# RMSNorm with SiLU on one core: loads and stores trade their issuing engines, and each is issued at another moment

## The chip, the cores and the metric

The kernel runs on one core of a Trainium2 chip, and the program uses no other. The metric is the time of one execution on the device, in microseconds (us). Times are medians over several executions; a profile belongs to one execution, and its "span" (first to last instruction) is some 2 us shorter than the time. All profiled executions used here are fast, with a granted clock of 1.0.

## The reference

```python
x: (8, 1024, 2048) float32, gamma: (2048,), eps = 1e-5
rms = sqrt(mean(x ** 2, axis=-1, keepdims=True) + eps)
out = gamma * x / rms
result = out * (1 / (1 + exp(-out)))          # SiLU, float32
```

The input is 67.1 MB, and so is the output.

## The kernel before

The 8192 rows are cut into 16 blocks of 512 rows. A block is one tile of 128 partitions by 4 rows of 2048 numbers (4.194 MB), loaded by one transfer, worked on in place, and stored by one transfer. Six such tiles exist. VectorE takes the sums of squares of two rows of a block and does all scaling; ScalarE takes the other two sums, the square root and the SiLU. The parts that the change touches:

```python
J = 4
BUFS, LEAD = 6, 6
...
pool = ctx.enter_context(tc.tile_pool(name="pool", bufs=BUFS))
...
def load(b):
    xt = pool.tile([P, J * d], f32, name="xt")
    nc.sync.dma_start(out=xt, in_=xb[b])            # SyncE issues loads
    blocks[b] = xt

def sums(b, after_first=()):
    # ... VectorE: two tensor_tensor_reduce (cut)
    for j in range(na):
        nc.scalar.activation(out=junk_a, in_=row(b, j), func=ACT.Square,
                             accum_out=ss[:, j:j + 1])
        if j == 0:
            for s in after_first:
                store(s)                            # behind the first Square of block b
    # ... ScalarE: Sqrt (cut)

def finish(b, halves=False):
    for j in range(J):
        # VectorE: row * rstd * gamma (cut); after each second row:
        #   ScalarE: Silu over two rows; if halves: store those two rows
        ...

def store(b):
    nc.scalar.dma_start(out=ob[b], in_=blocks[b])   # ScalarE issues stores
    if b + LEAD < nblk:
        load(b + LEAD)                              # waits on SyncE for that store's landing

# gamma: 8 KB into a borrowed tile of the pool, spread to all partitions by TensorE (cut)
for b in range(1, last - 1):
    sums(b + 1, after_first=[b - 1])
    finish(b)
    invert(b + 1)
store(last - 2)
finish(last - 1)
store(last - 1)
sums(last)
invert(last)
finish(last, halves=True)
```

Waits aren't written by hand: an instruction that touches a tile waits for the instruction or transfer that has to be done with it. The wait stands on the engine that issues: in the kernel before, SyncE waits for stores to land in ten of its loads, 222.1 us in all.

## Time and profile before

| | before |
|---|---|
| time, median (lowest to highest), 3 runs | 317.37 us (317.27 to 317.58) |
| span of the profiled execution | 316.3 us (its time: 318.03 us) |
| VectorE, ScalarE busy | 223.5 us, 223.8 us (71% each) |
| two DMA queues, share of 16 engines' span | 49.7% and 49.2% |
| load, issue to landing (median) | 42.0 us |
| store, issue to landing (median) | 35.2 us |

Two habits help in reading it. First, the view puts a packet's whole time and all its bytes down to the stretch in which it starts, so that a short stretch can exceed 1.00. The DMA share tells whether packets were in flight, and only the rate in GB/s tells whether bytes flow as fast as they can. Second, "issue to landing" is mostly time in a queue: a block needs 4.194 MB / 433 GB/s = 9.7 us of the DMA engines, not 42.

### The profile page before, as it was taken

What the parts mean: (1) busy time and instruction counts of PE and PEld (TensorE: products, weight loads), DVE (VectorE), ACT (ScalarE), POOL (GpSimd) and SP (SyncE); (2) the same over time, 40 slices, a digit from 0 to 9 for tenths busy, and PEclk for the clock granted to TensorE, in tenths of its full rate; (3) what the DMA queues carried; (4) which work ended last, traced back from release to release, by engine and by line L of the source; (5) the groups of instructions that cost most, each with busy time, mean ns of one, the idle gap of its engine ahead of it and who ended that gap; (6) DMA issues with size and microseconds to landing.
All of it is one profiled execution on the core that took longest, in us unless ns stands there. A gap on an engine that the chain in (4) does not pass through costs nothing.

```text
span 316.3 us, 444 instructions
## 1 busy us (share of the span) xinstructions
PE 2.1 (1%) x8; PEld 0.5 (0%) x8; DVE 223.5 (71%) x147; ACT 223.8 (71%) x144; POOL 0.2 (0%) x4
## 2 busy tenths in 40 slices
PE   0200000000000000000000000000000000000000
PEld 0000000000000000000000000000000000000000
DVE  0679499999493983939849397593966939993900
ACT  1357958999967777678676687676786776879540
POOL 0000000000000000000000000000000000000000
DMA  8999999999999999999999999999999999999996
GB/s 328 402 464 410 452 390 410 452 419 443 439 424 452 411 452 410 452 414 456 406 456 414 448 414 448 439 423 452 414 452 410 452 414 456 406 456 410 452 407 269
DMA packets 4763, 134.25 MB, mean 425 GB/s; under 512 B 532, under 2 KB 532, under 8 KB 536
## 3 DMA queue, kind: packets, MB, share of 16 engines
q1 hardware_dynamic: 2304, 67.11, 49.7%
q10 hardware_dynamic: 2456, 67.12, 49.2%
q14 instruction: 3, 0.02, 0.0%
HBM read 67.12 MB, written 67.11 MB: 424 GB/s over the span
## 4 chain that ended last, share of the span: by engine, by line
DMA 74%; DVE 14%; ACT 5%; issue 2%; DVEq 1%; ACTq 0%; SPq 0%
DMA xt<-in_x_dram 44%; DMA out_dram<-xt 30%; DVE xt L84 11%; ACT xt L88 3%; DVE junk_v L64 3%; ACT junk_a L68 1%; DVEq L164 1%; ACT L74 0%; ACT rms L74 0%; DVE rstd L79 0%; ACTq L93 0%; DVE ss L64 0%; SPq L52 0%; DVEq L64 0%; ACTq L74 0%
## 5 line engine op out<-in xcount | busy, mean ns | idle before, releaser
L84 DVE SCALAR_TENSOR_TENSOR xt<-xt,rstd,g 128x2048 f32<-128x2048 f32 x64 | 146.2, 2347 | 0.1
L88 ACT ACTIVATE xt<-xt 128x4096 f32<-128x4096 f32 x32 | 115.4, 3615 | 36.8 <-DVE xt L84 36.7
L64 DVE CUSTOM_DVE_ANT_0 junk_v<-xt 128x2048 f32<-128x2048 f32 x32 | 73.5, 2298 | 56.1 <-DMA xt<-in_x_dram 55.5
L68 ACT ACTIVATE junk_a<-xt 128x2048 f32<-128x2048 f32 x32 | 60.1, 1879 | 29.2 <-DMA xt<-in_x_dram 28.3
L74 ACT ACT_TABLE_LOAD x15 | 19.2, 1283 | 9.9 <-DVE ss L64 9.9
L88 ACT ACT_TABLE_LOAD x15 | 19.2, 1283 | 3.1 <-DVE xt L84 2.9
L79 DVE RECIPROCAL rstd<-rms 128x4 f32<-128x4 f32 x16 | 2.8, 172 | 11.3 <-ACT rms L74 11.3
L114 DVE COPY g<-junk_v 128x2048 f32<-128x2048 f32 x1 | 2.3, 2292 | 9.2 <-PE junk_v L112 9.2
L68 ACT ACTIVATION_READ_ACCUMULATOR junk_a<-xt 128x1 f32 x32 | 6.0, 186 | 0.0
L74 ACT ACTIVATE rms<-ss,eps_t 128x4 f32<-128x4 f32 x16 | 4.8, 297 | 1.2 <-DVE ss L64 1.1
L64 DVE DVE_READ_ACCUMULATOR2_ANT ss<- 128x1 f32 x32 | 4.5, 141 | 0.0
L112 PE MATMUL junk_v<-xt,ones 1*128 1x512 f32 x8 | 2.1, 1133 | 8.1 <-DMA xt<-in_gamma_dram 8.1
L107 ACT ACT_TABLE_LOAD x1 | 1.3, 1283 | 0.7 <-PEq L150 0.7
L105 DVE MEMSET ones<- 128x128 f32 x1 | 0.2, 165 | 0.8 <-PEq L150 0.8
L112 PEld LDWEIGHTS junk_v<-xt,ones 1*128 1x128 f32 x8 | 0.5, 306 | 8.1 <-issue 8.1
L107 ACT ACTIVATE junk_a<-ones 128x1 f32<-128x1 f32 x1 | 0.2, 174 | 0.0
L150 POOL MEMSET const-uint8-127<- 128x1 uint8 x1 | 0.1, 102 | 0.0
L150 POOL MEMSET const-bfloat16-1.0<- 128x1 bf16 x1 | 0.1, 101 | 0.0
L150 POOL MEMSET const-float32-0.0<- 128x1 f32 x1 | 0.1, 98 | 0.2 <-issue 0.2
L150 POOL MEMSET const-float32-1.0<- 128x1 f32 x1 | 0.1, 98 | 0.0
L106 DVE MEMSET eps_t<- 128x1 f32 x1 | 0.1, 59 | 0.0
## 6 DMA issues: line engine op xcount, KB each, us to landing
xt<-in_x_dram SPq DMA_DIRECT2D x16, 4096.0 KB, 42.0
out_dram<-xt ACTq DMA_DIRECT2D x15, 4096.0 KB, 35.2
out_dram<-xt ACTq DMA_DIRECT2D x2, 2048.0 KB, 10.4
xt<-in_gamma_dram ACTq DMA_DIRECT2D x1, 8.0 KB
```

What stands on the lines that cost most here:

```text
L64: nc.vector.tensor_tensor_reduce(out=junk_v, in0=row(b, j), in1=row(b, j), scale=1.0, scalar=0.0, op0=ALU.mult, op1=ALU.add, accum_out=ss[ ...
L68: nc.scalar.activation(out=junk_a, in_=row(b, j), func=ACT.Square, accum_out=ss[:, j:j + 1])
L74: nc.scalar.activation(out=rms, in_=ss, func=ACT.Sqrt, scale=1.0 / d, bias=eps_t)
L79: nc.vector.reciprocal(out=rstd, in_=rmss.pop(b))
L84: nc.vector.scalar_tensor_tensor(out=row(b, j), in0=row(b, j), scalar=rstds[b][:, j:j + 1], in1=g, op0=ALU.mult, op1=ALU.mult)
L88: nc.scalar.activation(out=blocks[b][:, cols], in_=blocks[b][:, cols], func=ACT.Silu)
L105: nc.vector.memset(ones, 1.0)
L107: nc.scalar.activation(out=junk_a[:, 0:1], in_=ones[:, 0:1], func=ACT.Square)
L112: nc.tensor.matmul(junk_v[:, c * w:(c + 1) * w], ones[k:k + 1, :], grow[k:k + 1, 0:w], start=True, stop=True)
L114: nc.vector.tensor_copy(out=g, in_=junk_v)
L150: nc = _bacc.Bacc("TRN2", target_bir_lowering=False, num_devices=1)
L164: with _tile.TileContext(nc) as tc:
```

## The change

The intent: the engine that waits for a store's landing shall be ScalarE, which issues the next load where it is needed, and a store shall go out as soon as its SiLU is done, from SyncE, which has nothing else to do. Loads are tied to landings: load b+3 stands behind the first Square of block b+1, "the block two in front of it".

```diff
-    BUFS, LEAD = 6, 6
+    BUFS = 6
...
+    Q = 4
+    w = d // Q
+    grow = singles.tile([P, w], f32)
...
     def load(b):
         xt = pool.tile([P, J * d], f32, name="xt")
-        nc.sync.dma_start(out=xt, in_=xb[b])
+        nc.scalar.dma_start(out=xt, in_=xb[b])
...
                 for s in after_first:
-                    store(s)
+                    load(s)
...
     def store(b):
-        nc.scalar.dma_start(out=ob[b], in_=blocks[b])
-        if b + LEAD < nblk:
-            load(b + LEAD)
+        nc.sync.dma_start(out=ob[b], in_=blocks[b])
...
-        for b in range(BUFS - 1):
+        for b in range(BUFS):
             load(b)
...
-        nc.scalar.dma_start(out=grow[0:P:P // Q, 0:w], ...)
+        nc.sync.dma_start(out=grow[0:P:P // Q, :], ...)
...
-        load(BUFS - 1)
...
         finish(0)
+        store(0)
...
         for b in range(1, last - 1):
-            sums(b + 1, after_first=[b - 1])
+            sums(b + 1, after_first=[b + 3] if BUFS <= b + 3 < nblk else [])
             finish(b)
+            store(b)
             invert(b + 1)
-        store(last - 2)
```

(The two half stores of the last block move from ScalarE to SyncE too.)

More of the change, by code (lines that the diff above doesn't have):

```diff
@@ L89, in finish @@
                 if halves:
-                    nc.scalar.dma_start(out=ob[b][:, cols], in_=blocks[b][:, cols])
+                    nc.sync.dma_start(out=ob[b][:, cols], in_=blocks[b][:, cols])
     def store(b):
-        nc.scalar.dma_start(out=ob[b], in_=blocks[b])
-        if b + LEAD < nblk:
-            load(b + LEAD)
+        nc.sync.dma_start(out=ob[b], in_=blocks[b])
     with tc.manual_schedule():
-        Q = 4
-        w = d // Q
-        grow = pool.tile([P, J * d], f32, name="xt")
-        for b in range(BUFS - 1):
+        for b in range(BUFS):
             load(b)
@@ L107 @@
         nc.scalar.activation(out=junk_a[:, 0:1], in_=ones[:, 0:1], func=ACT.Square)
-        nc.scalar.dma_start(out=grow[0:P:P // Q, 0:w],
-                            in_=bass.AP(tensor=gamma.tensor, offset=gamma.offset, ap=[[w, Q], [1, w]]))
+        nc.sync.dma_start(out=grow[0:P:P // Q, :],
+                          in_=bass.AP(tensor=gamma.tensor, offset=gamma.offset, ap=[[w, Q], [1, w]]))
         for c in range(Q):
             k = c * (P // Q)
-            nc.tensor.matmul(junk_v[:, c * w:(c + 1) * w], ones[k:k + 1, :], grow[k:k + 1, 0:w],
+            nc.tensor.matmul(junk_v[:, c * w:(c + 1) * w], ones[k:k + 1, :], grow[k:k + 1, :],
                              start=True, stop=True)
         nc.vector.tensor_copy(out=g, in_=junk_v)
-        load(BUFS - 1)
         last = nblk - 1
```

## The prediction

> **What bounds the kernel now.** I read the page first, for which engine is full. Its third part lists the DMA queues: packets, megabytes, and the time of their packets as a share of the span of 16 DMA engines.
>
> ```profile
> DMA  8999999999999999999999999999999999999996
> GB/s 328 402 464 410 452 390 410 452 419 443 439 424 452 411 452 410 452 414 456 406 456 414 448 414 448 439 423 452 414 452 410 452 414 456 406 456 410 452 407 269
> ...
> q1 hardware_dynamic: 2304, 67.11, 49.7%
> q10 hardware_dynamic: 2456, 67.12, 49.2%
> ```
>
> Two queues carry 67.1 MB each (the input once, the output once) and together fill 49.7 + 49.2 = 98.9% of the DMA engines' time; VectorE and ScalarE are each busy for only 71% (223.5 and 223.8 us). Every slice but the first and the last is at 90% or more. So the question is not who issues, but whether the DMA engines ever run dry, and at what rate they work. For that I asked for the rate in stretches of my choice: start, loads alone, first store, steady state, stores alone, end. The last two columns are the DMA share and GB/s.
>
> ```profile
> 0.00:12.00 12.00, 2.09 (x8) 0.55 (x8) 1.94 (x3) 1.46 (x2) 0.20 (x4) 1.00 0.87 350
> 12.00:36.00 24.00, 0.00 (x0) 0.00 (x0) 19.19 (x14) 17.37 (x12) 0.00 (x0) 1.00 1.01 437
> 36.00:44.00 8.00, 0.00 (x0) 0.00 (x0) 5.70 (x6) 6.85 (x10) 0.00 (x0) 1.00 1.00 385
> ...
> 142.00:219.50 77.50, 0.00 (x0) 0.00 (x0) 55.20 (x36) 56.41 (x36) 0.00 (x0) 1.00 1.00 433
> ...
> 278.20:300.00 21.80, 0.00 (x0) 0.00 (x0) 16.65 (x11) 16.81 (x10) 0.00 (x0) 1.00 1.00 433
> 300.00:308.00 8.00, 0.00 (x0) 0.00 (x0) 1.09 (x1) 3.83 (x2) 0.00 (x0) 1.00 0.95 409
> 308.00:313.00 5.00, 0.00 (x0) 0.00 (x0) 0.00 (x0) 0.00 (x0) 0.00 (x0) 1.00 0.99 426
> 313.00:316.30 3.30, 0.00 (x0) 0.00 (x0) 0.00 (x0) 0.00 (x0) 0.00 (x0) 1.00 0.08 35
> ```
>
> Loads alone run at 437 GB/s, loads and stores mixed at 433, stores alone at 433. The total is therefore about the same whatever the mix, and only stretches below some 432 GB/s can be won back. Each loses its length times (1 - rate/432): the start 12 x (1 - 350/432) = 2.3 us, the stretch in which the first store begins 8 x (1 - 385/432) = 0.9 us, 300 to 308 us 0.4 us, the end 0.1 + 3.3 x (1 - 35/432) = 3.1 us. That is 6.7 us in the whole span of 316.3 us, and 5.4 us of it are the start of the first transfer and the landing of the last.
>
> Last, the timeline in the steady state, which shows who waits for whom within a block (start, us, engine, what; in brackets the idle time before it and what ended it).
>
> ```profile
> 195.35 3.62 ACT L88 ACTIVATE xt<-xt 128x4096 f32<-128x4096 f32 x1 [0.91 <-DVE xt L84]
> ...
> 200.81 1.88 ACT L68 ACTIVATE junk_a<-xt 128x2048 f32<-128x2048 f32 x1 [1.85 <-DMA xt<-in_x_dram]
> 200.87 0.34 ACTq L93 DMA_DIRECT2D out_dram<-xt  x1
> ```
>
> The Square of the next block starts when its load lands; such Squares stand at 181.46, 200.81 and 220.16 us, so a block takes 19.35 us, which is 2 x 4.194 MB / 19.35 us = 433.5 GB/s: the DMA's own pace. The last Silu of a block ends at 195.35 + 3.62 = 198.97 us, 17.5 us after the landing at 181.46, and ScalarE then idles 1.85 us for the next landing. Its store is issued only at 200.87, behind that landing.
>
> **What the Trainium skill says.** The page "DMA: Bandwidth & Descriptors" bears on this in three places. Its section "Issuing engines are not separate DMA queues" says that DMAs begun by different engines run on the same 16 DMA engines and interleave; trading queues then gives no bandwidth. The trace agrees so far: two queues at 49.7% and 49.2% add to one full set. "Where 436 GB/s comes from" puts the ceiling of the ports at 435 GB/s; the 433 measured in the steady state is within 0.5% of it (the same section's limit of about 358 for HBM isn't what this trace shows with one core at work). "Queues, rings and completion order" says that each DMA engine takes turns between the queue rows with work, packet by packet. In the trace a block of loads takes about 9.7 us alone (4.194 MB at 433 GB/s) and 19.35 us beside stores, which fits equal turns. The same page, under "Anatomy of one DMA — SWDGE (gpsimd) path", says that waits on semaphores happen on the issuing sequencer before dispatch. No view of before tests this for a load on ScalarE, but it is the danger of the change: there, a load that waits for a buffer's old store holds up ScalarE's arithmetic too.
>
> **The change part by part.**
> (1) Stores move to SyncE, right behind the last Silu. In the steady state each goes 200.87 - 198.97 = 1.9 us earlier, store 0 about 4 us earlier (its Silu ends at 32.70 us, it was issued at 36.67). The DMA engines are full at both moments, so this reorders bytes and adds no room: 0 us.
> (2) Loads move to ScalarE. Ten of them stand in the loop behind a Square, where 13 of the 17 stores stood. An issue costs the sequencer about 0.33 us in either place (0.34 for a store in the timeline, 328 ns median for a load), and ScalarE issues 16 loads in place of 17 stores and gamma. ScalarE has 1.85 us idle per block. 0 us.
> (3) A load is now tied to a landing as well as to a free buffer. Do the queues run dry? Load b+3 is issued just behind the landing of block b+1, when block b+2 is still to come: one whole block, 19.35 us of work beside stores or 9.7 us alone. ScalarE would have to be that late before the load queue emptied. In the start-up it is late by the most: block 4's Square comes after block 2's Silu, at some 67 us, and load 6 with it (before: 61.4 us). By my count from the rates block 5 then still has about 0.8 of a block to load, so nothing empties.
> (4) Does load b+3 wait for store b-3? A buffer's round takes 6 x 19.35 = 116.1 us. Before: store 35.2 (median to landing) + load 42.0 + from landing to store issue 220.22 - 181.46 = 38.8, sum 116.0: closed, no slack, SyncE simply waits for the store. After: load 2 x 19.35 = 38.7, holding 19.35 + 17.6 = 36.9, which leaves 116.1 - 75.6 = 40.5 us for the store. With two stores in the queue it takes 35.2 us, at worst 2 x 19.35 = 38.7. So 2 to 5 us to spare: the wait should be over when ScalarE comes to it.
> (5) Gamma gets a tile of its own and goes out on SyncE at once. Before, VectorE's copy of gamma ended at 12.5 us, ahead of the first block at 13.1 us; loads precede it in a different queue in both kernels. Load 5 no longer waits for it, but four loads were queued in front anyway. 0 us.
> (6) The start of the stores. Store 0 now lands near 55 us, and store 1 can't be issued before its Silu ends at about 56 us; so the store queue starts up twice, where before it started once. If each start loses up to the 0.9 us seen at 36 to 44 us, this adds 0 to 0.9 us, and I take 0.2.
> (7) The end hangs on the landing of block 14 (258.88 us) and the compute behind it: last half store issued 304.77 - 258.88 = 45.9 us later, which no part changes. 0 us.
> Sum: 317.4 + 0.2 = 317.6 us.
>
> **The rivals.**
> A. The wait moves onto ScalarE and stops the arithmetic. For it: the spare time in (4) is only a few us. Against it: while ScalarE is stopped, stores b-3 to b-1 and load b+2 are queued, so the DMA engines work on; the loss comes only at the end, if the last stores are issued late. I put this at 1 to 3 us, 318.5 to 320.5.
> B. Earlier stores fill bubbles and the kernel gets faster. For it: up to 1.3 us of the 6.7 us (the stretches at 36 and 300 us) aren't start or end latency. Against it: the steady state is at 433 GB/s with none to fill. At best 316.
> C. The store queue, now shallower, runs empty in every block, and starting it again costs rate each time. For it: the dip at the first store. Against it: by (4) the store queue should stay close to two deep. If it cost 0.3 us on each of 12 blocks, 321.
>
> **Range and chances.** The centre is 317.6. B bounds it below at about 316, A above at about 319 to 320; executions agree within 0.1% (317.27 to 317.58). I give 316.0 to 319.4. Faster by 2% would be 311.0, that is 6.3 of the 6.7 us that are not at full rate, most of them fixed latency: 0.01. Slower by 2% is 323.7 and needs C at twice the size, or a stall that I don't see: 0.03. Within 2%: 0.96.
>
> **What would show it.** Right: the two queues still fill some 99% of the DMA engines, mixed stretches at 432 to 434 GB/s, Squares 19.35 us apart, and ScalarE idle for about 1.9 us per block until a load lands. Store issue to landing stays near 35 us, and load issue to landing falls from 42 to near 38.7 us. For (4): no wait on ScalarE's queue for a store's landing in the loop. Rival A shows as such waits and a last half store issued later than 305 us; B as a rate above 420 GB/s at 36 to 44 us; C as a store landing time near 20 us and a steady rate clearly below 433 GB/s. The prediction is wrong if the mixed rate itself depends on which queue holds the deeper backlog, for which before has no contrast.

## The result, and the profile after

The changed kernel takes 317.23 us (317.16 to 317.56, 6 runs), the kernel before on the same chip 317.48 us (317.27 to 317.81, 6 runs). The ratio is 0.9993, with a 95% interval of 0.998 to 1.0006: the same. A ratio here is always the mean time of one kernel's fast runs over the mean of the other's fast runs of the same rounds, so not quite the ratio of the medians quoted.

The page of the changed kernel: busy tenths and rate of the DMA engines in 40 slices, and the two queues.

```profile
DMA  8999999999999999999999999999999999999997
GB/s 334 408 458 408 391 458 408 458 408 458 408 459 408 459 408 453 412 458 412 453 412 453 420 445 424 445 420 445 428 437 428 441 433 433 441 424 441 424 418 314
...
q10 hardware_dynamic: 2304, 67.11, 49.8%
q1 hardware_dynamic: 2456, 67.12, 49.4%
```

The queues have traded names (q10, with 2304 packets, now carries the loads), and that is all: 49.8 + 49.4 = 99.2%, against 98.9%. The rate over the same stretches as before (the last two columns are DMA share and GB/s):

```profile
0.00:12.00 12.00, 2.09 (x8) 0.55 (x8) 1.89 (x3) 1.46 (x2) 0.20 (x4) 1.00 0.87 350
12.00:36.00 24.00, 0.00 (x0) 0.00 (x0) 19.24 (x14) 17.41 (x12) 0.00 (x0) 1.00 1.04 437
36.00:44.00 8.00, 0.00 (x0) 0.00 (x0) 5.74 (x6) 6.85 (x10) 0.00 (x0) 1.00 0.91 393
44.00:64.00 20.00, 0.00 (x0) 0.00 (x0) 19.97 (x13) 16.19 (x11) 0.00 (x0) 1.00 1.01 437
...
142.00:219.50 77.50, 0.00 (x0) 0.00 (x0) 55.20 (x36) 56.41 (x36) 0.00 (x0) 1.00 1.00 433
...
300.00:308.00 8.00, 0.00 (x0) 0.00 (x0) 1.24 (x1) 3.98 (x2) 0.00 (x0) 1.00 0.95 410
```

They are the same stretches with the same rates: 350, 437, 433, 410. Only the stretch of the first store moved, from 385 to 393 GB/s, and that is no reading: the same view gives this kernel 459 GB/s when the edges are moved by 1 us, to 37 and 45 us. Over 12 to 64 us the two kernels have 429 and 430 GB/s. The profiled span is 1.2 us shorter than before (315.1 against 316.3), but that execution of before took 318.03 us, some 0.6 us above the median of its kind, so no gain of 1.2 us is to be read from it.

In the steady state of the changed kernel, the timeline shows the same block as before:

```profile
195.99 3.62 ACT L91 ACTIVATE xt<-xt 128x4096 f32<-128x4096 f32 x1 [0.91 <-DVE xt L87]
...
201.46 1.88 ACT L71 ACTIVATE junk_a<-xt 128x2048 f32<-128x2048 f32 x1 [1.85 <-DMA xt<-in_x_dram]
201.47 0.33 ACTq L55 DMA_DIRECT2D xt<-in_x_dram  x1
```

ScalarE again ends its SiLU (195.99 + 3.62 = 199.61 us), idles 1.85 us, and starts the next Square when the load lands. The only difference is what follows the landing: a load on its queue where a store stood. The list of who waited for whom, in which the total, the number of times and the longest are given, confirms that ScalarE didn't pay for its new duty:

```profile
ACT xt L91 <- DVE xt L87: 39.2, 28, 3.6
ACT junk_a L71 <- DMA xt<-in_x_dram: 26.2, 11, 7.9
```

In the whole list no instruction of ScalarE waits for a store's landing, and the last half store is issued at 304.91 us (before: 304.77), not later than 305 us as rival A would have it.

### The profile page after: what moved, and what is told of

It reads as the page before. It is cut to its first block, busy times and chain, and to the rows that moved or that the text cites. A ratio compares the mean times of both kernels' runs of the same rounds, so it can differ in the third digit from the quotient of the medians.

```text
span 315.1 us, 438 instructions
## 1 busy us (share of the span) xinstructions
PE 2.1 (1%) x8; PEld 0.5 (0%) x8; DVE 223.6 (71%) x147; ACT 223.7 (71%) x144; POOL 0.2 (0%) x4
## 3 DMA queue, kind: packets, MB, share of 16 engines
q10 hardware_dynamic: 2304, 67.11, 49.8%
q1 hardware_dynamic: 2456, 67.12, 49.4%
## 4 chain that ended last, share of the span: by engine, by line
DMA 65%; DVE 18%; ACT 10%; issue 2%; DVEq 1%; ACTq 0%
DMA xt<-in_x_dram 65%; DVE xt L87 13%; ACT xt L91 6%; DVE junk_v L67 4%; ACT junk_a L71 2%; ACT L77 2%; DVEq L161 1%; ACT L91 0%; ACT rms L77 0%; DVE rstd L82 0%; DVE ss L67 0%; DVEq L67 0%; ACTq L77 0%
## 5 line engine op out<-in xcount | busy, mean ns | idle before, releaser
L91 ACT ACTIVATE xt<-xt 128x4096 f32<-128x4096 f32 x32 | 115.5, 3616 | 39.2 <-DVE xt L87 39.2
L67 DVE CUSTOM_DVE_ANT_0 junk_v<-xt 128x2048 f32<-128x2048 f32 x32 | 73.6, 2299 | 56.6 <-DMA xt<-in_x_dram 55.9
L71 ACT ACTIVATE junk_a<-xt 128x2048 f32<-128x2048 f32 x32 | 60.1, 1879 | 26.7 <-DMA xt<-in_x_dram 26.2
L109 PE MATMUL junk_v<-grow,ones 1*128 1x512 f32 x8 | 2.1, 1132 | 8.1 <-DMA grow<-in_gamma_dram 8.1
## 6 DMA issues: line engine op xcount, KB each, us to landing
xt<-in_x_dram ACTq DMA_DIRECT2D x16, 4096.0 KB, 38.7
out_dram<-xt SPq DMA_DIRECT2D x15, 4096.0 KB, 34.6
```

The lines of the kernel that those rows point to most:

```text
L67: nc.vector.tensor_tensor_reduce(out=junk_v, in0=row(b, j), in1=row(b, j), scale=1.0, scalar=0.0, op0=ALU.mult, op1=ALU.add, accum_out=ss[ ...
L91: nc.scalar.activation(out=blocks[b][:, cols], in_=blocks[b][:, cols], func=ACT.Silu)
L109: nc.tensor.matmul(junk_v[:, c * w:(c + 1) * w], ones[k:k + 1, :], grow[k:k + 1, :], start=True, stop=True)
```

## The experiments

My theory: the DMA engines' rate is the whole time. As long as each DMA engine has bytes queued, neither the issuing engine nor the moment of issue nor a wait on an engine with slack matters. The rivals are those of the prediction: the wait hurts on ScalarE (A), earlier stores win something that something else loses (B), starting a queue anew costs rate (C). Twelve kernels ran, in three batches of four; each was timed in 3 rounds against the kernel before on the same chip. The medians of before in the batches were 317.46, 317.62 and 317.53 us.

| kernel | median, us | ratio to before (95%) |
|---|---|---|
| no arithmetic, old issue | 317.53 | 0.9995 (0.9978 to 1.0011) |
| no arithmetic, new issue | 317.10 | 0.9987 (0.9972 to 1.0002) |
| before, stores early | 317.38 | 0.9993 (0.9978 to 1.0008) |
| changed, stores late | 317.61 | 1.0029 (0.9983 to 1.0074) |
| changed, 5 buffers | 317.60 | 1.0002 (0.9987 to 1.0017) |
| before, 5 buffers | 317.84 | 1.0003 (0.9984 to 1.0021) |
| changed, load one landing later | 329.16 | 1.0371 (1.0337 to 1.0404) |
| changed, store queue started anew | 331.33 | 1.0437 (1.0406 to 1.0469) |
| before, 4 buffers | 328.53 | 1.0343 (1.0320 to 1.0366) |
| changed, 4 buffers | 335.01 | 1.0524 (1.0450 to 1.0597) |
| changed, one queue, gamma behind the loads | 365.73 | 1.1507 (1.1486 to 1.1528) |
| changed, one queue, gamma apart | 320.52 | 1.0091 (1.0074 to 1.0107) |

### Is there anything beside the transfers? The arithmetic taken out

```diff
-        sums(0) ... finish(last, halves=True)
+        for b in range(nblk):
+            store(b)                       # old: loads on SyncE, stores on ScalarE
+        # new: store(b) on SyncE, then load(b + 3) on ScalarE
```

The output is x itself and wrong.

> All arithmetic between load and store is taken out (the output is wrong on purpose: it is x itself); loads on SyncE and stores on ScalarE as before. Theory (the DMA engines' rate is the whole time, everything else hides beside it): 134.2 MB at 433 GB/s plus some 3.5 us of start and landing, a span of 313 to 316 us, that is 0.988 to 1.0 of before. Rival (waits between arithmetic and transfers cost a few per cent that some order of issue could win back): clearly below, 305 us or less.

> The same without arithmetic, with loads on ScalarE and stores on SyncE (output wrong on purpose). Theory: as the other copy within 0.3%, since both queues feed the same DMA engines. Rival (the queue that carries the loads matters): they differ by over 0.5%.

Measured: 317.53 and 317.10 us. The span of the first is 315.9 us, above the 313 or so of my lowest expectation but inside the range. The page of the copy with the old issue:

```profile
DMA  8999999999999999999999999999999999999996
...
q1 hardware_dynamic: 2304, 67.11, 49.7%
q10 hardware_dynamic: 2312, 67.12, 49.2%
...
HBM read 67.12 MB, written 67.11 MB: 425 GB/s over the span
```

A kernel that computes nothing takes as long as either kernel. So all 224 us of work on VectorE and on ScalarE, and every wait between them, are hidden in both, and no other order of the arithmetic around these transfers can win more than noise. (Orders of the transfers themselves were tried only in these two forms, and smaller first or last transfers, which might shorten the start and the end, not at all.) The copies differ from each other by less than their intervals, though their transfers queue very differently (store issue to landing 42.7 us in one, 28.8 us in the other). This is the strongest single result: rival B is out for this change. Neither kernel has anything left above its own transfers.

### One part alone: the early stores

```diff
 # in the kernel before: store(b) no longer behind the Square of block b+2, but
             finish(b)
+            store(b)
             invert(b + 1)
```

> Part 1 of the change alone: each store right behind its last Silu, everything else as before (loads on SyncE when the old store has landed, stores on ScalarE). Theory: 0 us, within 0.4% of before; the round of a buffer shifts by about 1.9 us from holding to queueing. Rival (the earlier stores win something that the tied loads lose again): faster by 1 us or more.

Measured 0.9993, as foreseen. The opposite, early stores undone in the changed kernel:

```diff
     def store(b):
+        if b + 2 < nblk:       # 4 bytes of block b+2: can't go before that block has landed
+            nc.sync.dma_start(out=tick[0:1, 0:1], in_=blocks[b + 2][0:1, 0:1])
         nc.sync.dma_start(out=ob[b], in_=blocks[b])
```

> Part 1 undone in the changed kernel: ahead of each store SyncE copies 4 bytes of the block two behind it, so the store goes out only when that block has landed, as before the change. Theory: holding a buffer takes about 38.8 us again, 38.6 are left for the store, which takes 35 to 39, so ScalarE may wait a little for a store's landing; 0 to 0.5% slower than before. Rival (the earlier store is what keeps the change from losing): over 1% slower.

Measured 1.0029, with an interval that holds 1: three of four executions took 317.21 to 317.65 us, one 320.32 us, for which I have no cause. The list of waits now has 17.6 us in 6 waits of ScalarE for a store's landing, the little that the sum of the prediction foretold, and the rate at 142 to 219.5 us is still 433 GB/s. (The 4-byte copy also held up VectorE for 12.8 us in all, so this isn't quite the pure undoing.) So the moment of the store is worth nothing either way.

### Rival A: ScalarE made to wait

```diff
-    BUFS = 6
+    BUFS = 5
```

and for the kernel before BUFS, LEAD = 5, 5.

> The changed kernel with five buffers in place of six. Load b+3 then needs the buffer of block b-2, whose store is still on its way: by the sum of the prediction, 5 x 19.35 - 75.6 = 21 us are left for a store that takes about 35, so ScalarE has to stop for about 14 us in every block. Theory (while it is stopped two or three transfers are queued, so the DMA engines work on): +1 to +3 us in all, at the end, where the last stores come later; rival A in its strong form (ScalarE's wait costs its length, or part of it, per block): 10 blocks x several us, 340 us or more.

> The kernel before with five buffers in place of six: the same shortage of buffers, but the wait for the store stands on SyncE, where nothing else queues. Theory: 0 us, within 0.4% of before, some 1 to 3 us faster than the changed kernel with five buffers. Rival (five buffers are too few whoever waits): as slow as that one.

Measured 1.0002 and 1.0003. The waits of the changed kernel with five buffers, against those with six above:

```profile
ACT junk_a L71 <- DMA out_dram<-xt: 57.4, 10, 7.8
...
ACT xt L91 <- DVE xt L87: 12.7, 6, 3.6
...
ACT junk_a L71 <- DMA xt<-in_x_dram: 8.3, 1, 8.3
```

The wait of rival A is there now, for ten of the eleven loads that the loop issues, 57.4 us in total, and it costs nothing. Two things explain it. ScalarE had idled anyway: its waits for VectorE shrank from 39.2 to 12.7 us and those for loads from 26.2 to 8.3, together 44.4 us less. And while it stands, transfers are queued: by the trace's packet records the DMA engines were never idle from 36 to 300 us. I had expected 1 to 3 us at the end; none came. The wait itself was mis-sized too: 5.7 us per block where I had foretold about 14, because with fewer buffers the transfers also queue for a shorter time (medians to landing 24.9 us for a load and 26.2 us for a store, where the sum had 38.7 and 35). So rival A isn't merely absent from the changed kernel: with one buffer fewer it is present and harmless.

### How late may a load be? One landing later

```diff
-            sums(b + 1, after_first=[b + 3] if BUFS <= b + 3 < nblk else [])
+            sums(b + 1, after_first=[b + 2] if BUFS <= b + 2 < nblk else [])
```

> The changed kernel with each load tied to the landing of the block one in front of it, not two: load b+2 is issued when block b+1 has landed, so the load queue is empty at every landing. Theory (the tie is free only as long as a block is still queued behind the one that lands): now both queues run empty at times, some 10 us slower, 325 to 332 us, and the DMA share falls to about 95%. Rival (DMA engines are full anyway and stores fill the gap): within 1 us.

Measured 1.0371, a median of 329.16 us, as expected; the DMA share fell less than I thought, to 48.9 + 48.7 = 97.6%. The rate in two stretches of this kernel:

```profile
64.00:142.00 78.00, 0.00 (x0) 0.00 (x0) 53.56 (x36) 55.81 (x37) 0.00 (x0) 1.00 1.00 431
142.00:272.00 130.00, 0.00 (x0) 0.00 (x0) 86.24 (x57) 89.82 (x56) 0.00 (x0) 1.00 0.98 407
```

At first the stock of stores still hides the empty load queue; then the rate falls to 407 GB/s, where the changed kernel has 432 in the same stretch. In the packet records the load queue stands still for some 4 to 6 us at each of these landings, where in the changed kernel no pause of it from 20 us to its end reaches 1 us. The tie to a landing is free because it is two blocks in front, so that one whole block is queued when the next load is issued. One block in front, it costs 3.7%. A whole block isn't needed, though: with five buffers a load landed 24.9 us after its issue and a block came every 19.4 us, so it was issued only some 5.5 us ahead of the landing before it, and that cost nothing either.

### Rival C: the store queue started anew for every block

```diff
     def store(b):
+        if b > 0:              # 4 bytes into the block before: can't go before its store has landed
+            nc.sync.dma_start(out=blocks[b - 1][0:1, 0:1], in_=x2[0:1, 0:1])
         nc.sync.dma_start(out=ob[b], in_=blocks[b])
```

> The changed kernel with a transfer of 4 bytes ahead of each store, which writes into the previous block's buffer and so can't be issued before that block's store has landed: the store queue is at most one store deep and starts up anew for every block. Result right, as those buffers are loaded again or done with. Theory (the load queue fills the gaps): within 0.5% of before. Rival C (each start of the store queue costs 0.3 to 0.9 us): 4 to 13 us slower.

Measured 1.0437: my expectation was wrong, and by its number rival C was right. The rates say when:

```profile
64.00:128.00 64.00, 0.00 (x0) 0.00 (x0) 56.47 (x37) 49.22 (x31) 0.00 (x0) 1.00 1.00 432
128.00:272.00 144.00, 0.00 (x0) 0.00 (x0) 97.84 (x66) 101.39 (x68) 0.00 (x0) 1.00 1.00 409
```

Up to 128 us the stores start anew as well, but the load queue is deep, and the rate is 432 GB/s, the same as in the changed kernel. These three starts anew beside a deep load queue thus cost nothing. After 128 us the timeline shows what has happened:

```profile
169.31 0.25 SPq L97 DMA_DIRECT2D xt<-in_x_dram  x1
169.66 0.34 SPq L98 DMA_DIRECT2D out_dram<-xt  x1
171.63 0.33 ACTq L55 DMA_DIRECT2D xt<-in_x_dram  x1
172.02 1.88 ACT L71 ACTIVATE junk_a<-xt 128x2048 f32<-128x2048 f32 x1 [6.96 <-DMA xt<-in_x_dram]
```

The store (169.66) and the load (171.63) are now issued within 2 us of each other, once per block: the load waits on ScalarE for its buffer (here for the 4-byte write that follows that buffer's store, which adds to the effect), and the buffers are piled up in front of the slow store queue. Both queues are then about one block deep, and both start anew once per block. Yet idle DMA engines are not the main loss here: the share stays at 1.00 and only the GB/s fall, so the packets themselves take longer. In the packet records a full packet (32,768 bytes) takes 1.21 us in filled queues. From 142 to 219.5 us 88 packets, all in the 6.3 us after one of these issues, took 1.3 to 2.7 us; that adds up to 4.0 us of all sixteen engines, against 0.5 us of idle engines. Why they take longer isn't shown. My working had looked at the store queue alone and forgotten that slow stores starve the loads of buffers. Where only stores are left, the bare cost of one start can be read: they are issued at 284.31, 295.73 and 307.22 us, 11.45 us apart on average, where a block takes 9.7 us in a filled queue; some 1.8 us each, of which 0.3 us is the issue of the 4-byte transfer. About 8 of the 14 us that this kernel lost lie between 128 and 272 us (144 x (1 - 409/433)), the rest mostly in these last stores.

### Where the two orders part: four buffers

```diff
-    BUFS, LEAD = 6, 6                          # before
+    BUFS, LEAD = 4, 4
-    BUFS = 6                                   # changed
+    BUFS = 4
-  ... after_first=[b + 3] if BUFS <= b + 3 < nblk else []
+  ... after_first=[b + 2] if BUFS <= b + 2 < nblk else []
```

> The kernel before with four buffers. A round of four buffers at full rate is 4 x 19.35 = 77.4 us; the holding takes 38.8 of it, so 38.6 are left for one store and one load side by side, which take 19.35 each plus the start of each after the other's landing, some 2 to 2.5 us. Theory (a buffer's round decides, and only a queue that runs empty costs): both queues are one deep and run empty in turn, 325 to 335 us, estimate from my model 333. Rival (as with five buffers, DMA never notices): within 0.5%.

> The changed kernel with four buffers, each load tied to the landing one block in front of it (two in front isn't possible with four). Holding takes 36.9 us instead of 38.8, so a round has 1.9 us more for the transfers. Theory: 325 to 335 us as well, within 1% of the old order with four buffers and if anything faster by some us; here the earlier store would show its worth. Rival (a wait on ScalarE costs more than on SyncE once buffers are short): slower than the old order with four buffers by over 1%.

(The 2 to 2.5 us for a start, in the first text, fit the run before: its 4-byte write was issued at 169.31 us, and the load that waited for it at 171.63, which is 2.3 us.) Measured 328.53 and 335.01 us. The first is in its range (my model's 333 was 4 us too high). The second I got wrong: 1.0524 / 1.0343 = 1.0175, so the changed order is 1.7% slower than the old one (some 1.0 to 2.5% by the two intervals), where I had thought it equal or faster. The changed kernel with four buffers, in stretches, and below it two stretches of the old order with four:

```profile
60.00:72.00 12.00, 0.00 (x0) 0.00 (x0) 6.15 (x5) 10.03 (x6) 0.00 (x0) 1.00 0.94 401
72.00:142.00 70.00, 0.00 (x0) 0.00 (x0) 46.72 (x32) 46.63 (x32) 0.00 (x0) 1.00 0.97 412
142.00:272.00 130.00, 0.00 (x0) 0.00 (x0) 91.07 (x59) 91.08 (x59) 0.00 (x0) 1.00 1.00 417
...
300.00:318.00 18.00, 0.00 (x0) 0.00 (x0) 13.37 (x10) 13.42 (x10) 0.00 (x0) 1.00 0.88 379
```

```profile
60.00:72.00 12.00, 0.00 (x0) 0.00 (x0) 7.43 (x5) 11.31 (x7) 0.00 (x0) 1.00 0.99 429
...
300.00:318.00 18.00, 0.00 (x0) 0.00 (x0) 12.90 (x9) 12.80 (x9) 0.00 (x0) 1.00 0.98 422
```

In the two stretches between, the old order had 421 and 416 GB/s. So the loss isn't in the long steady stretch but before and after it. Early on a load that has to wait for a landing and its turn on ScalarE goes out later than one that leaves SyncE as soon as its buffer is free (load 6 at 97.13 us against 90.71, load 8 at 137.53 against 130.78, though not load 7). At the end no load is left, and the last half store goes out at 323.27 us against 318.35. This explanation fits the code and the issue times but was not taken apart by a run of its own, so it stays argued; above all, this pair differs in the tie too (one block in front, which alone cost 3.7% with six buffers), so the 1.7% isn't the price of the original change. The changed kernel's executions spread from 332.68 to 337.89 us; the longest is slow and is in the median but not in the ratio. The profiled execution was one of the two short ones, which are still 1.3% above the old order's median.

### Are two queues needed? Loads and stores in one

```diff
     def load(b):
         xt = pool.tile([P, J * d], f32, name="xt")
-        nc.scalar.dma_start(out=xt, in_=xb[b])
+        nc.sync.dma_start(out=xt, in_=xb[b])
```

> The changed kernel with the loads on SyncE as well, so that loads and stores are in one queue in program order, and ScalarE issues none. By count at least two transfers stay queued at each issue. Theory (only a supply of queued bytes matters, not the number of queues): within 0.5% of before, each load and each store taking some 9.7 us of its own. Rival (two queues side by side are needed for the mixed rate of 433 GB/s): over 2% slower.

Measured 1.1507, which looked like a clear win for the rival until I read the start of the timeline:

```profile
0.73 2.89 SPq L55 DMA_DIRECT2D xt<-in_x_dram  x6
...
3.65 0.63 SPq L105 DMA_DIRECT2D grow<-in_gamma_dram  x1
...
61.77 2.09 PE L109 MATMUL junk_v<-grow,ones 1*128 1x512 f32 x8 [61.77 <-DMA grow<-in_gamma_dram]
```

The experiment was confounded: gamma, 8 KB, stood behind six loads of 4.194 MB in the same queue and landed at 61.77 us, where the changed kernel has it at 8.14. Nothing could be scaled or stored before. Mended:

```diff
-        nc.sync.dma_start(out=grow[0:P:P // Q, :], ...)
+        nc.scalar.dma_start(out=grow[0:P:P // Q, :], ...)
```

> The single queue again, mended: in the first try gamma stood behind six loads of 4 MB in the same queue and VectorE waited for it until about 60 us. Now gamma goes out on ScalarE, and only loads and stores of blocks share SyncE's queue. Theory (a supply of queued bytes is what matters): most of the 48 us is gone, within 1% of before. Rival (two queues side by side are needed for the rate): still over 2% slower, with a steady rate clearly below 430 GB/s.

Measured 1.0091 (up to 1.0107 by its interval), just inside the theory's 1% but outside the 0.5% that I had given before the first try: 45 of the 48 us were gamma's place. What is left is small but real:

```profile
44.00:64.00 20.00, 0.00 (x0) 0.00 (x0) 19.97 (x13) 16.20 (x11) 0.00 (x0) 1.00 0.99 415
...
142.00:219.50 77.50, 0.00 (x0) 0.00 (x0) 54.23 (x36) 55.34 (x36) 0.00 (x0) 1.00 1.00 430
...
308.00:313.00 5.00, 0.00 (x0) 0.00 (x0) 0.00 (x0) 0.00 (x0) 0.00 (x0) 1.00 1.01 433
313.00:319.00 6.00, 0.00 (x0) 0.00 (x0) 0.00 (x0) 0.00 (x0) 0.00 (x0) 1.00 0.22 96
```

The rate where the first stores follow the loads is 415 GB/s instead of 437, which is about 1 us; the steady rate is 430 instead of 433, and the end trails off. The single queue is therefore nearly as good, not quite. Why the last 0.9% is lost wasn't tested. The first failure shows something that the change needed: when the loads went to ScalarE's queue, gamma had to leave it. That part of the diff looks like tidying; the single queue with gamma behind the six loads shows some 45 us for it.

## Why the prediction was right

The time lies in the predicted range (317.23 in 316.0 to 319.4; the centre of 317.6 was 0.4 us high), and most of its steps hold.

(1) Early stores, 0 us: shown from both sides, 0.9993 added to the old kernel and 1.0029 (interval holding 1) taken from the new.

(2) The trade of engines, 0 us: for the transfers alone shown by the two copies. With the arithmetic, the changed kernel and the old one with early stores differ in the engines, the tie and gamma's place, and both have a ratio of 0.9993; so these three together are worth nothing.

(3) Load queue not empty: load 6 was issued at 65.93 us (predicted some 67), and block 5 landed 19.35 us later, so that about a whole block was still to come where I had counted 0.8. The experiment with one landing later shows the edge, 12 us lost where the queue does run empty.

(4) The buffer's round: predicted load 38.7 us and store about 35 us; measured 38.7 and 34.6 us (medians), which leaves 40.5 - 34.6 = 5.9 us to spare, a little above the 2 to 5. No wait of ScalarE for a store was seen with six buffers. Five buffers brought it, as the sum said, but 5.7 instead of 14 us per block, and it cost 0 instead of 1 to 3 us.

(5) Gamma, 0 us: right as the change does it. The step undersold the part, as the single queue showed.

(6) Start of the stores, 0 to 0.9 us, taken as 0.2: the one term that was mis-sized. Store 1 was issued at 55.77 us, and the second start that I allowed for did come: the packet records have no store packet from 55.9 to 59.3 us. The loads filled that gap (no idle DMA engine, 437 GB/s at 44 to 64 us in both kernels), so it cost 0 us. Nor did three such starts beside a deep load queue in rival C's experiment (432 GB/s up to 128 us). The first start of the stores costs some 0.8 us in longer packets, but in both kernels alike. The measured difference to before is -0.25 us in the medians, which is noise.

(7) The end, 0 us: 410 against 409 GB/s at 300 to 308 us, and the last half store issued 304.91 - 259.52 = 45.4 us after block 14's landing (predicted 45.9).

Of the rivals, A and B fell as told above. (B's sign, a rate above 420 GB/s at 36 to 44 us, was too coarse to decide anything, as its 393 turns into 459 with a shift by 1 us; the times decide.) C fell for this change (steady rate 433, stores at 34.6 us), but its fear is sound where both queues are one block deep: that costs 3.4 to 5.2% with four buffers and 4.4% with forced starts. The closing caution, that the mixed rate might depend on which queue holds the backlog, is also answered: in the new copy the loads hold the deeper backlog (77.4 us to landing, stores 28.8), in the old order with five buffers the stores do (31.5 us, loads 24.5), and both take the same time in total.

## What to carry to other kernels

When the DMA engines carry the whole time, ask only two things of a change of issue: does each moment still have bytes queued, in one queue while the other is started (here some 5 us of transfers were enough, none was not), and does anything small and early end up behind something large in the same queue. A cheap test comes first: take the arithmetic out and time the transfers; if that kernel is as slow as yours, no reordering of the arithmetic will help, and what is left to gain lies in the transfers themselves. The change that is worth nothing with six buffers took another tie with four and was then 1.7% slower than the old order, so judge an order of issue where buffers are short if it is to be used there.

## What the Trainium skill lacked or had wrong

- "DMA: Bandwidth & Descriptors", section "Where 436 GB/s comes from", says that for transfers between HBM and SBUF the HBM limit of about 358 GB/s binds. With one core at work this case ran at 433 GB/s of loads and stores together for most of its span (425 GB/s over the whole copy), so for one core the 435 of the ports is the limit that fits. The same section points to 425 GB/s measured for one large load, so it is this one sentence that misleads for a core that works alone.
- The same page, "Issuing engines are not separate DMA queues", says that issuing from several engines only saves the sequencer's time. The section doesn't say what the order within a queue can cost: 8 KB behind six loads in one queue landed at 61.77 us instead of 8.14, and all transfers in one queue were 0.9% slower than in two. "Perfetto Trace Analysis", section "DMA Optimizations", suggests one engine for inputs and another for outputs; these runs agree and put the number 0.9% to it.
- "DMA: Bandwidth & Descriptors", section "Anatomy of one DMA — SWDGE (gpsimd) path", places waits on the issuing sequencer. The runs agree for SyncE and ScalarE, which issue here (57.4 us of ScalarE waiting for stores with five buffers), and add that such a wait cost 0 us while transfers were queued.
- No page that I read says how deep the queues must be. Here a load issued some 5.5 us ahead of the landing before it was early enough (changed kernel with five buffers, ratio 1.0002), and one issued at that landing was not (407 GB/s).
- No page that I read says that packets can take longer in the microseconds after a shallow queue starts anew: 1.3 to 2.7 us instead of 1.21 us in rival C's experiment, with the DMA share at 1.00.
